# A hybrid GLA/MLA encoder layer: the order of the first loads, eight places in the last projection sweep's timetable, and the maxima at both edges of attention

## The chip, the cores and the metric

The kernel runs on one core of one Trainium2 chip. The core has five engines with a queue each: TensorE (PE, matmuls and transposes), VectorE (DVE), ScalarE (ACT), GpSimd (POOL) and SyncE (SP), which issues most DMAs here. Each queue runs in order. The metric is the device time of one execution in microseconds (us); the time of a kernel is the median of its runs.

## The reference, cut to what matters

One encoder layer on a sequence of 2048 positions and a model width of 1024, all in float32:

```
h = x @ w_in                                   # one projection, columns split between two groups
group A: bidirectional gated linear attention (4 heads), per-head RMSNorm, times silu(gate)
group B: cq, ckv, kr, gate                     # 256, 128, 64 and 512 columns of h
  q = rms_norm(cq) @ w_uq, k_nope and v from rms_norm(ckv) @ w_ukv, rotary parts of q and kr
  s = q_nope . k_nope + q_rope . k_rope        # (query, key) scores, no mask
  p = softmax(s);  o = p @ v;  o * silu(gate)
out = layer_norm(alpha * x + concat(A, B) @ w_out)
```

The softmax is taken as exp(s - max s) over its sum, so each block of queries needs the maximum over all keys before its first exponential.

## The kernel before, in words

**Split numbers.** Every product is made of three matmuls: an operand is split into a high part (`hi`, L364, an ACT copy into the matmul type) and a low part (`lo`, L371, the difference, on DVE or POOL), and high*high, high*low and low*high are added in PSUM (`mm3`, L419).

**Sweep A** (`sweep_a`, L616) goes over the 16 chunks of 128 positions from the last to the first and makes group A's chunked attention. At its head the transposed x of chunk 15 is loaded in two halves and split, then 13 pieces of the weights of A follow in three column groups (`A_GROUPS`: 288, 384 and 384 columns), each split as it lands; `ident`, `wgf` (the gate's second weight) and `wgm` (a column of factors) are loaded behind the second group; `wg` is made from them on DVE (L669). Then x of chunk 14 is loaded and split. All these splits stand in one order per engine (`worder`). The first chunk's three products run in `step(0, ...)`; `lr` (the low-rank gate input) comes from the first, `lrT` is its transpose, `z` (L891) the gate product, which needs `lrTs` and `wg`, and `za` the chain of ACT and DVE steps behind it. The tiles of these steps (pool `g1`) lie in the memory that the weight stage (`sta`) leaves.

**Sweep C** (`sweep_c`, L1100) goes over the chunks again, two to a step, eight steps, and makes group B's projections and finishes group A. Its order is a timetable: every action has a place (step + offset in `PLACE_C`; `PLACE_C_FIRST` and `PLACE_C_LAST` replace it for the first and last step), all actions are sorted by place, and each engine's queue follows that order. A pair of offsets is for the even and the odd chunk of a step. The actions that matter here: `xh` and `xl` (high and low part of x of a chunk, into one of the two halves of `xch` and `xcl`; `xl` is on POOL), `ipa` to `ipd` (the mixed projection of a chunk in four parts of six matmuls, into `ipm`; in the last 8 of the 24 the low part of x is read), `pz` (the gate product of a step in eight parts, which reads both halves of `xch` and `xcl`), `gm1` to `gm4` (its silu: three ACT steps and one on DVE), `Ob` (the state part of group A's output, PE, which reads `MMb` and `qlb` that POOL makes), `og` (DVE, the last reader of `Ob`), `krfa` (POOL, the key's rotary sum), `krsh` (ACT, its high part), `pq` (the queries' product). `pz`, `Ob` and `pq` share two PSUM buffers in turn (tag `gp`), so each waits for the last reader of the one before the last.

The weights of sweep C (`load_ws`, L459) are split in eight pieces; high and low parts and the raw pieces share 17 buffers.

**Attention** (`attention`, L1507) has 16 blocks (4 heads times 4 blocks of 512 queries); each takes the 2048 keys in 8 score tiles of two PSUM banks. It also runs by places (`PLACE`, `PLACE_LAST` for the last block; the unit is one score tile): `scores` (10 matmuls into one of two buffers `pS`), `copy` (ACT, to `s` in SBUF), `smax` (DVE, two maxima of 512 columns into `rm`), at the block's end `tmax` (PE transposes), `rmax` (DVE), `bmax` (PE, spreads the maximum into `mb`), then `sub` (DVE), `exp`, `phi` (ACT), `plo` (POOL) and `pv` (PE, 6 matmuls into `o`). The buffer of a score tile is free when both its copy and its maximum have read it. In block 0 the maxima read the copies; in later blocks they read PSUM:

```
                src = s if i == 0 else ps
```

The output projection follows; its first matmuls (`po`) use the `pS` buffers that the last block leaves.

Of the kernel before, what the change touches and what calls it, by code (L numbers as in the profile page):

```python
# [9 lines left out]
F32 = mybir.dt.float32  # L10
# [85 lines left out]
    yc=16.9,  # L96
)
PLACE_LAST = dict(
    sub=(9.67, 8.74, 8.38, 6.77, 10.45, 3.53, 9.53, 5.55),
    exp=(10.14, 9.35, 10.49, 8.31, 13.01, 14.59, 17.1, 18.05),  # L100
# [158 lines left out]
    MMl=(-0.109, 0.558),  # L259
    krfa=(-0.119, 0.94),  # L260
    krsl=(0.252, 1.09),
# [9 lines left out]
    gm1=0.643,  # L271
    gm2=0.686,
    gm3=0.706,
    gm4=0.804,
    sgm=1.056,
# [10 lines left out]
    ipd=(0.042, 0.445),  # L286
    Ob=(-0.03, 0.299),
    tm=(0.495, 1.083),
# [30 lines left out]
    qrTl=(1.081, 2.186),  # L319
    xl=(-0.244, 0.038),  # L320
    M=(-0.531, -0.11),
# [35 lines left out]
class K:  # L357
# [100 lines left out]

    def load_ws(self, pool, srcs, ncols, tag, on_pool=()):  # L459


        names = lambda p: [f"{tag}{p}{k}" for k in range(NK)]
        raw = [pool.tile([P, ncols], F32, tag=tag, name=n) for n in names("r")]
        for r, src in zip(raw, srcs):
            self.w_load = self.nc.sync.dma_start(r, src).ins
        yield
        wh = [pool.tile([P, ncols], F32R, tag=tag, name=n) for n in names("h")]
        W = []
        for k, n in enumerate(names("l")):
            wl = pool.tile([P, ncols], F32R, tag=tag, name=n)  # L470
            self.hi(wh[k], raw[k])
# [144 lines left out]
    def sweep_a(self):  # L616
        tc, nc, ins, cp = self.tc, self.nc, self.ins, self.cp
        with ExitStack() as ctx:
# [6 lines left out]
            rmask = wp.tile([P, H, P], F32, name="rmask")  # L625
            wgm = wp.tile([98, 1], F32, name="wgm")
            wg = wp.tile([98, H, P], F32R, name="wg")
# [17 lines left out]
            with tc.tile_pool(name="sta", bufs=1, reuse_waits="tile") as sta:  # L645
                xf = self.load_x(NCH - 1, "xa", 1, 2)
                xcur = self.split_x(xp, xf, NCH - 1, "xa", "dve", 2)
                wgf = sta.tile([98, H * P], F32, name="wgf")
                wgh = sta.tile([98, H * P], F32R, name="wgh")
                wdone, worder = [], {}  # L650
                for g, (c0, n) in enumerate(A_GROUPS):
                    k = 0
                    for m in W_PIECES[g]:
                        st = sta.tile([P, m, n], F32, name=f"was{g}_{k}")
                        nc.sync.dma_start(st, ins[f"wA{g}"][:, k:k + m])
                        ks, cs = slice(k, k + m), slice(c0, c0 + n)
                        with self.in_order(worder):
                            for e in [slice(j, j + 1) for j in range(m)] if g == 0 else [slice(0, m)]:
                                kh, kl = wah[:, ks, cs][:, e], wal[:, ks, cs][:, e]
                                ops = self.hi(kh, st[:, e]), self.lo(kl, st[:, e], kh)  # L660
                        k += m
                        wdone.append(ops)
                    if g == 1:
                        nc.sync.dma_start(self.ident, ins["ident"])
                        nc.sync.dma_start(wgf, ins["wg"])
                        nc.sync.dma_start(wgm, ins["wgm"])
                with self.in_order(worder):
                    self.hi(wgh, wgf)
                    nc.vector.scalar_tensor_tensor(wg.rearrange("p h d -> p (h d)"), wgh.bitcast(F32), wgm[:, 0:1],  # L669
                                                   wgf, ALU.mult, ALU.add)  # L670
                xnext = self.split_x(xp, self.load_x(NCH - 2, "xa", 1, 2), NCH - 2, "xa", "dve", 2)
                nc.sync.dma_start(rmask, ins["rmask"])
                nc.sync.dma_start(mask, ins["mask"])
# [8 lines left out]
            run = lambda n, i: [0 for _ in getattr(self, "ga_" + n)(ch[i])]  # L682
            ch[0]["x"], ch[1]["x"] = xcur, xnext

# [14 lines left out]
            self.first_lr = wdone[7][0]  # L699
            step(0, {(1, 7): [("lrT", "cur")]})  # L700
            run("bst", 0)
# [42 lines left out]
    def products(self, d, g, after=lambda g, k: None):  # L744

        nc, c, i, g1 = self.nc, d["c"], d["i"], d["g1"]
        c0, n = A_GROUPS[g]
        xh, xl = d["x"]
        if i == 0 and g == 2:
            pt = self.gp.tile([P, 1024], F32, tag="gp", name=f"ipa{c}_{g}")  # L750
        else:
            pt = self.ip.tile([P, 512], F32, tag="ip", name=f"ipa{c}_{g}")
        d["pt", g] = pt
        for k in range(NK):
            wh, wl = self.wa[k]
            self.mm3(pt[:, :n], xh[:, k, 0], xl[:, k, 0], wh[:, c0:c0 + n], wl[:, c0:c0 + n],
                     start=(k == 0), stop=(k == NK - 1))
            if k < NK - 1:
                after(g, k)
            yield k  # L760
        if i == 0 or i > 3:
            for n in (("lr", "q2"), ("k2", "v1"), ("v3",))[g]:
                for _ in getattr(self, "ga_" + n)(d):
                    pass
# [303 lines left out]
    def late_gates(self):  # L1068
# [7 lines left out]
        self.wabs_l = bc.tile([P, 2, H, P], F32R, name="wabs_l")  # L1076
        wm = self.load_ws(self.wm, [ins["wB"][k, :, 512:960] for k in range(NK)], 448, "wm")
        wz = self.load_ws(self.wz, [ins["wB"][k, :, 960:1472] for k in range(NK)], 512, "wz")
        next(wm)
# [427 lines left out]
    def attention(self):  # L1507
# [4 lines left out]
        with ExitStack() as ctx:  # L1512
# [19 lines left out]

            def scores(i, j):


                d = stt[i]
                qh, ql, rh, rl = d["q"]
                ps = d["ps", j] = pS.tile([P, 2, QB], F32, tag="pS", name=f"pS{i}_{j}")
                for e in range(2):
                    kh, kl, kr = (t[:, 2 * j + e, :P] for t in (self.ckvT_h, self.ckvT_l, self.kr))  # L1540
# [11 lines left out]
            def smax(i, j):  # L1552

                d = stt[i]
                s = d["s"][j]
                ps = d.pop(("ps", j))
                src = s if i == 0 else ps
                if j == 0:
# [408 lines left out]
def layouts(inputs):  # L1967
# [19 lines left out]
    wg, bg = wg.reshape(32, H * P), bg.reshape(1, H * P)  # L1987
    a["wg"] = np.concatenate([wg, wg, wg, bg, bg], axis=0)
    wgm = np.zeros((98, 1), np.float32)
    wgm[64:96] = -1.0  # L1990
    wgm[97] = -1.0
    a["wgm"] = wgm
    a["gn_col"] = g["gla_norm_g"][0].reshape(P, 1)
# [41 lines left out]
```

## Time and profile before

| | us |
|---|---|
| median of 3 runs (lowest, highest) | 1308.29 (1307.52, 1310.21) |
| the profiled execution | 1306.76 |
| its span, first to last instruction | 1304.7 |
| PE busy | 1284.8 |
| DVE, ACT, POOL busy | 961.9, 817.2, 785.9 |

Sweep A fills the span to about 370 us, sweep C to about 610, attention to about 1130, and the output projection the rest. A row of the timeline has the start, the duration, engine, source line, operation, written and read tile, shape and count, and in brackets the idle time of the engine before it with what ended it. In the view of waits a row has the total, the count and the longest wait. The rows of stretches have, for each engine, the busy time and in parentheses the number of instructions, then the granted TensorE clock, the DMA share and the GB/s. A busy PE is not PE at its peak: matmuls overlap, and the idle times counted before them are a little shorter than the distance that the starts show.

### The profile page before, as it was taken

To read this page: it belongs to the slowest core of one execution; us is meant where nothing else is said; L and a number is where in the kernel's file an instruction comes from. 1 tells how busy PE (TensorE), PEld (TensorE's weight loads), DVE (VectorE), ACT (ScalarE), POOL (GpSimd) and SP (SyncE) were. 2 spreads that over 40 slices of the span, in tenths; PEclk is the share of its full clock that TensorE was granted. 3 is DMA by queue.
4 is the path that set the end of the run, shared out by engine and by line. 5 is a ranking of instruction groups with operands and counts; after the bars stand their busy time and mean duration, and the time that the engine had idled before them with its cause. 6 is when DMAs were issued, how large, how long until landed. Compare 5 with 4: busy or idle time off the path is not lost.

```text
span 1304.7 us, 19969 instructions
## 1 busy us (share of the span) xinstructions
PE 1284.8 (98%) x7082; PEld 1131.1 (87%) x7082; DVE 961.9 (74%) x1706; ACT 817.2 (63%) x1334; POOL 785.9 (60%) x494
## 2 busy tenths in 40 slices
PE   7999999999999999999999999999999999999997
PEld 7999999999999999999788888888888887888886
DVE  6966675656675555555888888888888888469997
ACT  6765655566676566564778787878888888511110
POOL 0143333242467667661488888889999999844441
PEclk9999999999999999999999999999999999999999
DMA  8132313131475555656301111121123210366662
GB/s 285 62 101 54 94 53 94 49 88 59 155 247 194 187 178 200 207 176 209 90 1 41 41 42 41 41 62 60 57 71 101 47 41 9 121 203 202 214 196 97
DMA packets 105908, 145.81 MB, mean 112 GB/s; under 512 B 16743, under 2 KB 59375, under 8 KB 105809
## 3 DMA queue, kind: packets, MB, share of 16 engines
q1 hardware_dynamic: 97744, 142.41, 34.8%
q0 software_dynamic: 672, 2.10, 0.4%
q8 instruction: 56, 0.92, 0.3%
q10 hardware_dynamic: 7392, 0.03, 0.3%
q14 instruction: 44, 0.35, 0.1%
HBM read 94.14 MB, written 50.36 MB: 111 GB/s over the span
## 4 chain that ended last, share of the span: by engine, by line
PE 91%; DVE 2%; ACT 2%; issue 1%; POOL 0%; SPq 0%; DMA 0%; DVEq 0%; ACTq 0%
PE pz L1210 7%; PE ipm L1281 5%; PE o L421 5%; PE o L423 5%; PE o L422 5%; PE pS L1541 4%; PE pS L1544 4%; PE pS L1543 4%; PE pS L1545 4%; PE pS L1542 4%; PE ipa L421 4%; PE ipa L422 4%; PE ipa L423 4%; PE po L421 2%; PE po L423 2%; PE po L422 2%
## 5 line engine op out<-in xcount | busy, mean ns | idle before, releaser
L373 POOL TENSOR_TENSOR pl<-s,ph 128x1024 fp32r<-128x1024 f32 x128 | 307.0, 2413 | 67.0 <-ACT ph L367 61.7
L1563 DVE TENSOR_TENSOR rm<-pS,rm 128x512 f32<-128x512 f32 x210 | 144.9, 690 | 44.7 <-ACT s L1550 39.6
L1550 ACT ACTIVATE s<-pS 128x1024 f32<-128x1024 f32 x128 | 131.4, 1027 | 68.2 <-PE pS L1545 66.2
L1587 DVE TENSOR_TENSOR s<-s,mb 128x1024 f32<-128x1024 f32 x128 | 151.2, 1213 | 9.1 <-PE mb L1581 9.0
L1039 POOL TENSOR_TENSOR Us<-Us,cw 128x512 f32<-128x512 f32 x16 | 20.0, 1248 | 228.5 <-DVE Us L1037 190.0
L367 ACT ACTIVATE ph<-s 128x1024 fp32r<-128x1024 f32 x128 | 135.0, 1056 | 18.3 <-PE o L423 17.8
L1591 ACT ACTIVATE s<-s 128x1024 f32<-128x1024 f32 x128 | 131.4, 1050 | 13.4 <-DVE s L1587 13.4
L421 PE MATMUL ipa<-wah,xah 128*128 128x384 f32 (+1 forms) x384 | 130.0, 339 | 6.5 <-ACT wah L367 6.4
L422 PE MATMUL ipa<-wal,xah 128*128 128x384 f32 (+1 forms) x384 | 125.7, 327 | 0.0
L423 PE MATMUL ipa<-wah,xal 128*128 128x384 f32 (+1 forms) x384 | 125.2, 326 | 0.0
L1541 PE MATMUL pS<-qh,ckvT_h 128*128 128x512 f32 x256 | 103.7, 405 | 0.7 <-ACT s L1591 0.4
L421 PE MATMUL o<-ph,vh 128*128 128x512 f32 x256 | 102.6, 401 | 0.0
L423 PE MATMUL o<-ph,vl 128*128 128x512 f32 x256 | 101.3, 396 | 0.0
L1544 PE MATMUL pS<-rh,krs 128*128 128x512 f32 x256 | 101.2, 395 | 0.0
L422 PE MATMUL o<-pl,vh 128*128 128x512 f32 x256 | 101.1, 395 | 0.0
L1543 PE MATMUL pS<-qh,ckvT_l 128*128 128x512 f32 x256 | 100.9, 394 | 0.0
L1545 PE MATMUL pS<-rl,krs 128*128 128x512 f32 x256 | 100.7, 393 | 0.0
L1542 PE MATMUL pS<-ql,ckvT_h 128*128 128x512 f32 x256 | 100.6, 393 | 0.0
L1614 DVE TENSOR_TENSOR ap<-ap,s 128x512 f32<-128x512 f32 x120 | 83.1, 693 | 2.7 <-ACT s L1591 0.8
L373 POOL TENSOR_TENSOR ol<-of,oh 128x512 fp32r<-128x512 f32 x32 | 43.0, 1345 | 64.7 <-ACT oh L367 64.7
L421 PEld LDWEIGHTS ipa<-wah,xah 128*128 128x128 f32 x384 | 73.4, 191 | 7.6 <-ACT wah L367 6.8
L422 PEld LDWEIGHTS ipa<-wal,xah 128*128 128x128 f32 x384 | 73.5, 191 | 0.9 <-DVE wal L373 0.4
(325 smaller groups left out, 3839.4 us busy)
## 6 DMA issues: line engine op xcount, KB each, us to landing
xcf<-xT_dram SPq DMA_DIRECT2D x16, 512.0 KB, 5.4
xr<-x_dram SPq DMA_DIRECT2D x16, 512.0 KB, 5.3
out_dram<-rr SPq DMA_DIRECT2D x32, 256.0 KB, 2.0
xaf<-xT_dram SPq DMA_DIRECT2D x14, 512.0 KB, 4.3
oib<-oi_s SPq DMA_DIRECT2D x16, 256.0 KB, 4.0
qdb<-qd_s SPq DMA_DIRECT2D x16, 256.0 KB, 4.2
SU<-su_s SPq DMA_DIRECT2D x16, 256.0 KB, 4.4
ub<-u_s SPq DMA_DIRECT2D x16, 256.0 KB, 4.6
```

The source lines that it names most:

```text
L367: return nc.scalar.activation(dst, src, AF.Copy).ins
L373: return e.tensor_tensor(dst, src, hi.bitcast(F32), ALU.subtract).ins
L421: mm(out, ah, bh, start=start, stop=False)
L422: mm(out, ah, bl, start=False, stop=False)
L423: mm(out, al, bh, start=False, stop=stop)
L1541: mm(ps[:, e], kh, qh, start=True, stop=False)
L1542: mm(ps[:, e], kh, ql, start=False, stop=False)
L1543: mm(ps[:, e], kl, qh, start=False, stop=False)
L1544: mm(ps[:, e], kr, rh, start=False, stop=False)
L1545: mm(ps[:, e], kr, rl, start=False, stop=True)
L1563: V.tensor_tensor(d["rm"], src[:, e], d["rm"], ALU.max)
L1587: V.tensor_tensor(s, s, d["mb"][:, None, :].to_broadcast([P, 2, QB]), ALU.subtract)
```

## The change

1. **First loads.** The halves of chunk 15's x are loaded and split in the weights' order: first half, two weight pieces, second half, two pieces. `wgm` becomes a 513th column of `wg`'s input, so its DMA goes, and `wgf` is loaded behind all weight pieces. x of chunk 14 is loaded behind it; its split is written down after the first chunk's step. In that step `lrT` comes after the sixth k of the second product instead of after the eighth, and the copy `q2` after the second product instead of the first.
2. **`load_ws`**: all eight high parts are written down ahead of the low parts.
3. **Sweep C's places.** First step: `krfa` of chunk 0 later (behind `MMl`, `qlb` of chunk 0 and `Sf2` of chunk 1 on POOL); `gm2` to `gm4` later (behind `xh` of chunk 2 on ACT; `gm4` behind `og` of chunk 0 on DVE). Last step: `Ob` of chunk 14 behind `ipc` of chunk 14 on PE; `xl` of chunk 15 later (behind `qlb`, `MMl` and `krfa` of chunk 15 on POOL). Its new place, 7.64, lies behind `ipc` and `ipd` of chunk 15 (7.42, 7.445) and the first two parts of the last `pz` (7.572, 7.578) and ahead of the third (7.707): those products now read the low part that chunk 13 left in that half of `xcl`, and the third part of `pz` reads the new one.
4. **Attention's edges.** The last maximum of block 0 (tile 7) reads PSUM and stands ahead of its copy; `bmax` of block 0 goes between the two halves of block 1's second score tile, which is put down as two halves of five matmuls; the maxima of block 1's first four tiles read the copies. In block 15 the last maximum stands ahead of its copy, and that copy goes behind `phi` of (14, 5) and the copy `yc` of block 13 on ACT.

```diff
+PLACE_FIRST = dict(bmax=2.01, max=(1.21,) * 7 + (0.72,))
 PLACE_LAST = dict(
+    max=(1.21,) * 7 + (0.72,),
+    copy=(0.73,) * 7 + (1.0,),
...
-    krfa=(-0.119, 0.94),
+    krfa=(-0.02, 0.94),
...
-    gm2=0.686,
-    gm3=0.706,
-    gm4=0.804,
+    gm2=0.815,
+    gm3=0.82,
+    gm4=0.83,
...
-    Ob=(-0.03, 0.299),
+    Ob=(0.0, 0.299),
...
-    xl=(-0.244, 0.038),
+    xl=(-0.244, 0.64),
...
+        if high_first:
+            for h, r in zip(wh, raw):
+                self.hi(h, r)
         for k, n in enumerate(names("l")):
             wl = pool.tile([P, ncols], F32R, tag=tag, name=n)
-            self.hi(wh[k], raw[k])
+            if not high_first:
+                self.hi(wh[k], raw[k])
...
+                        if g == 0 and k in (0, NK // 2):
+                            xs = slice(k, k + NK // 2)
+                            nc.sync.dma_start(xf[:, xs], ins["xT"][NCH - 1][:, xs])
+                            with self.in_order(worder):
+                                self.hi(xcur[0][:, xs, 0], xf[:, xs])
+                                self.lo(xcur[1][:, xs, 0], xf[:, xs], xcur[0][:, xs, 0])
...
                     if g == 1:
                         nc.sync.dma_start(self.ident, ins["ident"])
-                        nc.sync.dma_start(wgf, ins["wg"])
-                        nc.sync.dma_start(wgm, ins["wgm"])
+                nc.sync.dma_start(wgf, ins["wg"])
                 with self.in_order(worder):
-                    self.hi(wgh, wgf)
-                    nc.vector.scalar_tensor_tensor(wg.rearrange("p h d -> p (h d)"), wgh.bitcast(F32), wgm[:, 0:1],
-                                                   wgf, ALU.mult, ALU.add)
-                xnext = self.split_x(xp, self.load_x(NCH - 2, "xa", 1, 2), NCH - 2, "xa", "dve", 2)
+                    self.hi(wgh, wgf[:, :H * P])
+                    nc.vector.scalar_tensor_tensor(wg.rearrange("p h d -> p (h d)"), wgh.bitcast(F32),
+                                                   wgf[:, H * P:], wgf[:, :H * P], ALU.mult, ALU.add)
+                xnext = self.load_x(NCH - 2, "xa", 1, 2)
...
-            step(0, {(1, 7): [("lrT", "cur")]})
+            step(0, {(1, 5): [("lrT", "cur")]})
+            ch[1]["x"] = self.split_x(xp, xnext, NCH - 2, "xa", "dve", 2)
...
-            for n in (("lr", "q2"), ("k2", "v1"), ("v3",))[g]:
+            for n in ((("lr", "q2"), ("k2", "v1"), ("v3",)) if i else (("lr",), ("q2", "k2", "v1"), ("v3",)))[g]:
...
-                src = s if i == 0 else ps
+                src = s if NP * i + j < NP - 1 or NP <= NP * i + j < NP + 4 else ps
...
-                p = PLACE_LAST.get(f, PLACE[f]) if i == nb - 1 else PLACE[f]
+                p = {nb - 1: PLACE_LAST, 0: PLACE_FIRST}.get(i, {}).get(f, PLACE[f])
...
-                    put(t, scores, i, j)
+                    if (i, j) == (1, 1):
+
+                        put(t, scores, i, j, (0,))
+                        put(t + 0.02, scores, i, j, (1,))
+                    else:
+                        put(t, scores, i, j)
```

More of the change, by code (lines that the diff above doesn't have):

```diff
@@ L457, in load_w, with load_ws @@
         return wh, wl
-    def load_ws(self, pool, srcs, ncols, tag, on_pool=()):
+    def load_ws(self, pool, srcs, ncols, tag, on_pool=(), high_first=False):
         names = lambda p: [f"{tag}{p}{k}" for k in range(NK)]
@@ L625, in sweep_a @@
             rmask = wp.tile([P, H, P], F32, name="rmask")
-            wgm = wp.tile([98, 1], F32, name="wgm")
             wg = wp.tile([98, H, P], F32R, name="wg")
@@ L645, in sweep_a @@
             with tc.tile_pool(name="sta", bufs=1, reuse_waits="tile") as sta:
-                xf = self.load_x(NCH - 1, "xa", 1, 2)
-                xcur = self.split_x(xp, xf, NCH - 1, "xa", "dve", 2)
-                wgf = sta.tile([98, H * P], F32, name="wgf")
+                xf = self.xfp.tile([P, NK, P], F32, tag="xf", name=f"xaf{NCH - 1}", bufs=2)
+                xcur = [xp.tile([P, NK, 1, P], F32R, tag=f"x{p}", name=f"xa{p}{NCH - 1}", bufs=2) for p in "hl"]
+                wgf = sta.tile([98, H * P + 1], F32, name="wgf")
                 wgh = sta.tile([98, H * P], F32R, name="wgh")
@@ L682, in sweep_a @@
             run = lambda n, i: [0 for _ in getattr(self, "ga_" + n)(ch[i])]
-            ch[0]["x"], ch[1]["x"] = xcur, xnext
+            ch[0]["x"] = xcur
             def step(i, steps):
@@ L1076, in late_gates @@
         self.wabs_l = bc.tile([P, 2, H, P], F32R, name="wabs_l")
-        wm = self.load_ws(self.wm, [ins["wB"][k, :, 512:960] for k in range(NK)], 448, "wm")
-        wz = self.load_ws(self.wz, [ins["wB"][k, :, 960:1472] for k in range(NK)], 512, "wz")
+        wm = self.load_ws(self.wm, [ins["wB"][k, :, 512:960] for k in range(NK)], 448, "wm", high_first=True)
+        wz = self.load_ws(self.wz, [ins["wB"][k, :, 960:1472] for k in range(NK)], 512, "wz", high_first=True)
         next(wm)
@@ L1531, in fetch, with scores @@
                         nc.sync.dma_start(q[-1][r].bitcast(F32), src[h])
-            def scores(i, j):
+            def scores(i, j, es=(0, 1)):
                 d = stt[i]
                 qh, ql, rh, rl = d["q"]
-                ps = d["ps", j] = pS.tile([P, 2, QB], F32, tag="pS", name=f"pS{i}_{j}")
-                for e in range(2):
+                if es[0] == 0:
+                    d["ps", j] = pS.tile([P, 2, QB], F32, tag="pS", name=f"pS{i}_{j}")
+                ps = d["ps", j]
+                for e in es:
                     kh, kl, kr = (t[:, 2 * j + e, :P] for t in (self.ckvT_h, self.ckvT_l, self.kr))
@@ L1555, in smax @@
                 s = d["s"][j]
-                ps = d.pop(("ps", j))
-                src = s if i == 0 else ps
+                ps = d["ps", j]
+                src = s if NP * i + j < NP - 1 or NP <= NP * i + j < NP + 4 else ps
                 if j == 0:
@@ L1987, in layouts @@
     wg, bg = wg.reshape(32, H * P), bg.reshape(1, H * P)
-    a["wg"] = np.concatenate([wg, wg, wg, bg, bg], axis=0)
+    wg = np.concatenate([wg, wg, wg, bg, bg], axis=0)
     wgm = np.zeros((98, 1), np.float32)
@@ L1991, in layouts @@
     wgm[97] = -1.0
-    a["wgm"] = wgm
+    a["wg"] = np.concatenate([wg, wgm], axis=1)
     a["gn_col"] = g["gla_norm_g"][0].reshape(P, 1)
```

## The prediction

> **What bounds the kernel now.** I read the busy times of the page first.
>
> ```profile
> span 1304.7 us, 19969 instructions
> ## 1 busy us (share of the span) xinstructions
> PE 1284.8 (98%) x7082; PEld 1131.1 (87%) x7082; DVE 961.9 (74%) x1706; ACT 817.2 (63%) x1334; POOL 785.9 (60%) x494
> ```
>
> TensorE is the bound: 1304.7 - 1284.8 = 19.9 us of the span are all that it does not work. The change removes no matmul, so it can only move these holes or make new ones. PE's rows in the view of waits say where they are:
>
> ```profile
> PE ipa L421 <- ACT wah L367: 6.4, 2, 6.0
> PE mx L1569 <- DVE rm L1563: 0.9, 2, 0.6
> PE mb L1581 <- DVE mc L1574: 0.8, 1, 0.8
> PE z L891 <- ACT lrTs L367: 0.7, 1, 0.7
> PE Ob L1439 <- POOL qlb L373: 0.6, 1, 0.6
> ...
> PE pS L1541 <- ACT s L1591: 0.4, 1, 0.4
> PE pS L1541 <- DVE rm L1563: 0.3, 1, 0.3
> ```
>
> The start holds 6.4; below it single waits under 1 us stand at just the places that the change touches. So I go from place to place, and ask at each what is late next. Rows of the timeline, by engine, carry this.
>
> **Start.** ACT, DVE, PE, and then the stretches of PE's `ipa` matmuls:
>
> ```profile
> 4.64 0.63 ACT L367 ACTIVATE xah<-xaf 128x512 fp32r<-128x512 f32 x1 [0.31 <-DMA xaf<-xT_dram]
> 5.46 0.78 ACT L367 ACTIVATE wah<-was 128x288 fp32r<-128x288 f32 x2 [0.19 <-DMA was<-wA_dram]
> ```
> ```profile
> 20.01 1.14 ACT L367 ACTIVATE xah<-xaf 128x512 fp32r<-128x512 f32 x2
> 21.38 0.60 ACT L367 ACTIVATE q<-ipa 128x512 f32<-128x512 f32 x1 [0.24 <-DVE wg L669]
> ```
> ```profile
> 16.80 3.89 DVE L373 TENSOR_TENSOR wal<-was,wah 128x768 fp32r<-128x768 f32 x5 [0.88 <-ACT wah L367]
> 20.60 0.74 DVE L669 SCALAR_TENSOR_TENSOR wg<-wgh,wgm,wgf 98x512 fp32r<-98x512 f32 x1
> ```
> ```profile
> 22.85 0.66 PE L891 MATMUL z<-lrTs,wg 98*128 98x128 f32 x4 [0.74 <-ACT lrTs L367]
> ```
> ```profile
> 8.40:13.20 4.80, 4.72 (x18) 4.52 (x19) 0.00 (x0) 0.00 (x0) 1.00 1.03 351
> 13.20:17.50 4.30, 4.30 (x25) 4.18 (x24) 0.18 (x1) 0.27 (x2) 1.00 1.04 365
> ```
>
> The first weight's high part starts at 5.46, behind the second half of x at 4.64; with their order exchanged it can start 5.46 - 4.64 = 0.8 sooner, and so the first matmul. All bytes still come, though, and the last weights set when the first product ends. What leaves their way is `wgf`: 98 x 512 x 4 = 200,704 bytes, at the second stretch's 365 GB/s an estimated 0.55 us. So DVE's low parts (16.80 + 3.89 = 20.69) end 0.55 sooner, at 20.14; `wg` is now last behind them, 0.74, and done at about 20.9. The copies of `q`, `k`, `VV` and `lrTs` lie in memory of the weight stage and so wait for `wg`'s end, as the row at 21.38 shows; PE's 0.74 at `z` is their last, `lrTs`. With `lrT` earlier, `z` can come soon after 20.9 instead of at 22.85. But PE's next work is chunk 14's product, and its x, whose split (1.14 on ACT, as much on DVE) stood ahead of these copies, is now written down behind the step. If ACT gets it done while it waits for `wg`, product and `z` are both sooner, by an estimated 1.3 at most (the 1.14, and about half of the 0.24 that ACT waited); if it comes behind the copies (from 20.9 some 1.8, then 1.14, so till 23.8), PE waits there for what it gained at `z`, and may lose up to 0.4. Of -1.3 to +0.4 I take **-0.5**, what the loads alone give. In `load_ws` the high parts come ahead of lows that ACT need no longer wait for; matmuls without a hole cover this: **0**; uncovered, `gm1` would be what gains or loses, and it waits for PE.
>
> **Sweep C, first step.** ACT, then PE:
>
> ```profile
> 394.05 1.04 ACT L367 ACTIVATE xch<-xcf 128x1024 fp32r<-128x1024 f32 x1
> ```
> ```profile
> 395.61 0.35 PE L1438 MATMUL Ob<-MMb,qhb 128*128 128x256 f32 x1 [0.31 <-DVE gm L1224]
> ```
>
> `Ob` of chunk 1 needs the `gp` buffer that `gm4` reads last, and PE already waits 0.31 for it. The change puts ACT's copy of chunk 2 (1.04) ahead of `gm2` and `gm3`, so `gm4` ends 1.04 later and nothing else is late first: **+1.0**. Ends: 0 if something else holds `Ob` of chunk 1 as long already, which the 0.31 put down to `gm` speaks against, and +1.3 if `og` of chunk 0, now ahead of `gm4` on DVE, holds that too.
>
> **Sweep C, last step.** The two waits of `Ob` on PE:
>
> ```profile
> 577.75 0.33 PE L1439 MATMUL Ob<-MMb,qlb 128*128 128x128 f32 x1 [0.64 <-POOL qlb L373]
> ...
> 583.56 0.39 PE L1438 MATMUL Ob<-MMb,qhb 128*128 128x256 f32 x1 [0.42 <-POOL MMb L373]
> ```
>
> Both go: 0.64 (chunk 14, six `ipc` matmuls now stand ahead of it) and 0.42 (chunk 15, whose `qlb` and `MMl` lose `xl`'s place ahead of them on POOL). What is late next, on DVE and PE:
>
> ```profile
> 586.45 1.13 DVE L1465 SCALAR_TENSOR_TENSOR og<-Ob,rg_r,ub 128x128 f32<-128x128 f32 x4
> ```
> ```profile
> 588.19 0.28 PE L421 MATMUL pq<-cqT_h,wabs_h 128*128 128x256 f32 x1
> ```
>
> `og` of chunk 14 ends at 586.45 + 1.13 = 587.58, and `pq`, which needs its `gp` buffer, starts at 588.19, only 0.61 behind. PE would reach `pq` 1.06 sooner and then wait 1.06 - 0.61 = 0.45; and as `Ob` of chunk 14, moved behind `ipc`, starts `og`'s chain later by those matmuls, most of the 0.61 goes too. I take **-0.2**; ends -1.06 and 0.
>
> `xl` of chunk 15 is the new cost. POOL's `xl` (of chunk 14's place; all have one shape) and `krfa` of chunk 15, then PE in the last `pz`:
>
> ```profile
> 578.34 2.41 POOL L373 TENSOR_TENSOR xcl<-xcf,xch 128x1024 fp32r<-128x1024 f32 x1
> ```
> ```profile
> 594.38 0.33 POOL L1315 TENSOR_TENSOR krf<-krf,rope 128x64 f32<-128x64 f32 x1 [4.67 <-DVE rope L1490]
> ```
> ```profile
> 595.50 0.28 PE L1210 MATMUL pz<-xcl,wzh 128*128 128x256 f32 x1
> ...
> 595.86 0.28 PE L1210 MATMUL pz<-xcl,wzh 128*128 128x256 f32 x1
> ```
>
> `xl` overwrites the half of `xcl` that the first two parts of `pz` read, so POOL can't begin before the last of these reads, at 595.50, is over (595.78); the third part's first read of `xcl` is at 595.86 and now needs `xl`'s result. 595.78 + 2.41 = 598.2; PE's queue has nothing between that can go on, so the hole is 598.2 - 595.86 = 2.3, and an estimated 0.2 for two hand-overs: **+2.5**. `krfa`, put ahead of `xl`, ends at 594.71, in time. Ends: 0, if the third part isn't held, and 2.9, with hand-overs of 0.3 each (the smallest waits of the rows above). In the first step `krfa` of chunk 0 only changes its place among POOL's work (0.33 for such a sum); `krsh` on ACT waits for it, and `tm` on PE later still: **0**, up to 0.3 either way if `tm` were what PE meets next.
>
> **Attention's first edge.** DVE, PE, then a stretch (PE, PEld, DVE, ACT, POOL, busy us and instructions):
>
> ```profile
> 640.09 1.42 DVE L1563 TENSOR_TENSOR rm<-pS,rm 128x512 f32<-128x512 f32 x2 [0.40 <-ACT s L1550]
> ...
> 648.20 2.21 DVE L1563 TENSOR_TENSOR rm<-pS,rm 128x512 f32<-128x512 f32 x3
> ```
> ```profile
> 650.54 0.39 PE L1541 MATMUL pS<-qh,ckvT_h 128*128 128x512 f32 x1
> ```
> ```profile
> 635.00:649.20 14.20, 13.49 (x58) 10.38 (x57) 13.60 (x17) 14.06 (x15) 8.90 (x4) 1.00 0.01 1
> ```
>
> By the waits shown first, the edge's holes are 0.3 (`mx`, 0.9 less the 0.6 of the last edge), 0.8 (`mb`), 0.4 and 0.3 (`pS`): 1.8, and an estimated 2.5 with the 0.2 by which, at the `mx` below, a hole lengthens the distance of starts, for each of four. The change fills `mb`'s with half a score tile and takes the maximum away from `mx`'s path. What limits next is the exponentials' side: ACT works 14.06 of the 14.2 from 635.0 on, and DVE 13.60, so `sub`, `exp` and the copies don't come sooner than their own sum lets them; the maximum of (1, 4) at 648.20, which still reads PSUM, frees a buffer that PE takes at 650.54, 0.9 behind the 649.6 at which its two operations (1.4) end. So PE gains no more than that 0.9 and the little by which the chain starts sooner. And the copy of tile 7 now comes after its maximum, where 640.09 shows the reverse wait (0.40 for the copy of the same tile): the two are never side by side on one tile. I take **-1.0**; ends -2.5 and -0.3 (`mx`'s hole alone). The Trainium skill, "PSUM — Partial Sum Buffer", section "PSUM bank collisions raise a hardware error", says that two engines must not touch one bank at a time, reads among it; the trace agrees as far as the 0.40 goes. Were copy and maximum free to overlap, by that page's rule undone, the sum's -1.0 would be an estimated -1.2, and the time 1309.1.
>
> **Attention's last edge.** DVE and PE:
>
> ```profile
> 1100.16 1.42 DVE L1563 TENSOR_TENSOR rm<-pS,rm 128x512 f32<-128x512 f32 x2 [0.90 <-ACT s L1550]
> ```
> ```profile
> 1100.69 0.40 PE L423 MATMUL o<-ph,vl 128*128 128x512 f32 x1
> 1101.72 0.63 PE L1569 MATMUL mx<-ident,rm 128*128 128x128 f32 x4 [0.64 <-DVE rm L1563]
> ```
>
> The maximum of (15, 7) no longer waits 0.90 for its copy, so `mx`'s 0.64 goes (0.8 by starts: 1101.72 - 1100.69 = 1.03, less the 0.2 or so that lies between overlapping matmuls' starts): **-0.8**, ends -0.8 and 0. The copy, now behind a high part and `yc`, is due only at its `sub` and at `po`, which needs the buffer after many `pv`.
>
> **Sum:** -0.5 + 1.0 - 0.2 + 2.5 - 1.0 - 0.8 = +1.0. On the profiled execution (1306.76, that is its span and 2.06 around it) this gives 1307.8. The median of the runs, 1308.29, is 1.53 above that execution; on it the sum gives **1309.3**.
>
> **Rivals.** *No hole at `xl`.* If the third part of `pz` is not held, the sum loses 2.5, and with DVE a little ahead at `og` a further 0.86: +1.0 - 2.5 - 0.9 = -2.4, 1305.9; with the start's and the first edge's better ends (-0.8, -1.5) as far as 1303.6. For it: all gains stand where the waits are. Against: both `pz` rows read `xcl`, and one matmul has 256 columns, which are both chunks. Chance 0.23.
>
> *The hole slows what follows it* (the other side). In the stretch from 8.40, behind the 6.0 us wait, 18 matmuls of 288 columns took 4.72; at the second stretch's 4.30 for 25 of 384 they would have taken 18 x 288 x 4.30 / (25 x 384) = 2.3. So PE runs at half its pace for some 4.7 us after a long hole, though the granted clock shows 1.00 in both rows. Price 2.4, 1311.7; it decides if more than 1.6 of it comes. Against it: no hole of about 1 us later in the trace is followed by such matmuls, and 2.5 is nearer to these than to 6. Chance 0.15. The Trainium skill, "TensorE: Matmul & The Clock Gate", section "Part 1: The HAM clock gate (the "warmup" mystery)", gives half clock after an idle window of about 3.4 us, and as long for getting out of it: by that page 2.5 us of idle would not do.
>
> *The change doesn't do what it says at the start*: the split of chunk 14's x comes behind the copies and PE waits for it instead, +0.4 for -0.5; with the first edge giving its 0.3 alone, since PE waits at (1, 5) and (1, 6) for what it gained before, the sum is +1.0 + 0.9 + 0.7 = +2.6, 1310.9, on the border of slower. Chance 0.12.
>
> **How the numbers follow.** A measurement of this kernel can tell about 0.2%, 2.6 us. Forecast 0.50, its own range 1307.0 to 1310.9 (start and first edge each at an end). Faster: three quarters of the first rival and 0.03 of the forecast's tail, 0.20. Slower: the second rival and half the third, with 0.04 of the forecast's tail, 0.25. The rest, 0.55, is within. The range cuts about one in ten at each side: from 1304.4, inside the first rival, to 1312.4, the second with the start at its bad end.
>
> **What would show it.** After: a hole of 2.4 us on PE at a `pz` matmul put down to POOL `xcl`; `Ob` of chunk 1 waiting 1.3 for `gm`; no wait at the two last `Ob` but one at `pq` for `og`; no `mb` and `mx` waits, and new ones on `pS` until about 650; `z` at about 22.3. The prediction is wrong if `xl` comes between without a hole, if matmuls behind it run at half pace, or if a wait appears at a place not named here.

## The result, and the profile after

| | median us (lowest to highest, runs) | ratio to the kernel before (95% interval) |
|---|---|---|
| before | 1307.90 (1306.64 to 1310.21, 4) | |
| changed | 1316.64 (1315.10 to 1317.86, 4) | 1.0067 (1.0053 to 1.0082) |

The change costs 8.7 us, on the slower side and above the range of the prediction (1304.4 to 1312.4). The span of the profiled execution went from 1304.7 to 1314.0, 9.3 more.

The head of the changed kernel's page:

```profile
span 1314.0 us, 19954 instructions
## 1 busy us (share of the span) xinstructions
PE 1289.5 (98%) x7082; PEld 1133.8 (86%) x7082; DVE 970.1 (74%) x1706; ACT 816.6 (62%) x1334; POOL 789.5 (60%) x494
```

PE's busy time is 4.7 us longer for the same 7082 matmuls, so some of them ran slower; the idle time grew from 19.9 to 24.5, another 4.6. PE's rows in the view of waits say where the second half is:

```profile
PE ipa L424 <- ACT wah L370: 5.0, 1, 5.0
PE pS L1555 <- ACT ph L370: 3.7, 1, 3.7
PE pz L1222 <- DVE wzl L376: 2.5, 1, 2.5
PE pz L1222 <- POOL xcl L376: 2.2, 1, 2.2
PE pqr L424 <- ACT oT L1487: 0.8, 1, 0.8
```

Of the kernel before's waits, those at `mx` (last edge), `mb`, `z` and `Ob` are gone, as meant. In their place stand three of over 2 us. The third, for `xcl`, was forecast; the one for `wzl` and the one at `pS` were not. The slower matmuls are found by stretches (PE, PEld, DVE, ACT, POOL, then the granted clock): just behind the wait for `wzl`, just behind that for `xcl`, just behind that at `pS`, and a little later.

```profile
380.10:381.50 1.40, 1.34 (x6) 1.34 (x7) 1.40 (x6) 0.37 (x2) 1.40 (x3) 0.50 0.00 0
599.90:601.00 1.10, 1.04 (x8) 1.04 (x9) 0.00 (x0) 0.00 (x0) 0.00 (x1) 1.00 0.55 178
657.40:659.00 1.60, 1.54 (x4) 1.28 (x5) 1.55 (x3) 1.60 (x2) 1.60 (x2) 0.50 0.00 0
665.00:667.00 2.00, 2.00 (x10) 1.63 (x9) 0.85 (x2) 1.94 (x3) 1.69 (x1) 1.00 0.00 0
```

Behind two of the three holes the granted clock is 0.50. A ledger shows what each place is worth. It compares the start of the same matmul in both traces (after less before), and so adds up to what PE has lost by then:

| up to | after less before | step | what lies there |
|---|---|---|---|
| 358.71 (`Op`, end of sweep A) | -1.75 | -1.75 | the start |
| 378.5 to 384.5 (`pz`, first step of C) | +2.3 | +4.0 | hole for `wzl` 2.5, then 1.5 at half clock |
| 395.61 (`Ob` of chunk 1) | +1.75 | -0.5 | its wait for `gm` is gone |
| 577 to 594 (last step of C) | +1.7 | 0.0 | `Ob`'s waits gone (-1.1), a new one for `oT` (+1.1) |
| 595.86 (`pz`) | +4.09 | +2.4 | hole for `xcl` |
| 648 (first edge) | +2.7 | -1.4 | `mx`, `mb`, `pS` |
| 650.54 (`pS`, tile (1, 6)) | +6.9 | +4.2 | the hole at `pS` |
| 655 | +9.6 | +2.7 | half clock behind it |
| 1101.72 (`mx`, last edge) | +8.8 | -0.8 | the last edge |
| 1250 | +9.2 | +0.4 | output projection |

So most gains came about; two holes that the prediction did not have, with the clock behind them, are 4.0 + 6.9 = 10.9 us.

**Where the two holes come from.** Both lead to DVE. The low parts of the last weights, eight operations of one shape, before and after:

```profile
371.58 5.99 DVE L373 TENSOR_TENSOR wzl<-wzr,wzh 128x512 fp32r<-128x512 f32 x8
```
```profile
369.02 11.08 DVE L376 TENSOR_TENSOR wzl<-wzr,wzh 128x512 fp32r<-128x512 f32 x8
```

They begin 2.6 us sooner and end 2.5 later. The last two of them, and what POOL did at that time in the changed kernel:

```profile
374.85 5.25 DVE L376 TENSOR_TENSOR wzl<-wzr,wzh 128x512 fp32r<-128x512 f32 x2
```
```profile
374.29 1.37 POOL L1427 TENSOR_TENSOR SU<-Sf,cw 64x512 f32<-64x512 f32 x1
375.73 1.37 POOL L1419 TENSOR_TENSOR Sf<-Sf,cw 64x512 f32<-64x512 f32 x1
377.07 1.27 POOL L376 TENSOR_TENSOR MMb<-SU,MMb 128x512 fp32r<-128x512 f32 x1
378.30 1.25 POOL L376 TENSOR_TENSOR qlb<-qdb,qhb 128x512 fp32r<-128x512 f32 x1
```

Two operations that take 0.69 each alone last from 374.85 to 380.10. The single operations end 0.55 behind a POOL operation: POOL's row ends at 375.66 and the first of them at 376.2, POOL's at 379.55 and the last at 380.10. The last began at 376.3 and lasted 3.81, through three operations of POOL (those at 375.73, 377.07 and 378.30) that follow each other without a gap. The same picture at attention's first edge, DVE and POOL of the changed kernel:

```profile
644.30 2.81 DVE L1577 TENSOR_TENSOR rm<-s,rm 128x512 f32<-128x512 f32 x2 [0.26 <-ACT s L1564]
647.03 2.35 DVE L1601 TENSOR_TENSOR s<-s,mb 128x1024 f32<-128x1024 f32 x2
649.29 3.50 DVE L1577 TENSOR_TENSOR rm<-s,rm 128x512 f32<-128x512 f32 x2
652.71 2.15 DVE L1628 TENSOR_TENSOR ap<-ap,s 128x512 f32<-128x512 f32 x3
...
655.90 2.21 DVE L1577 TENSOR_TENSOR rm<-pS,rm 128x512 f32<-128x512 f32 x3
```
```profile
643.44 2.39 POOL L376 TENSOR_TENSOR pl<-s,ph 128x1024 fp32r<-128x1024 f32 x1 [12.69 <-ACT ph L370]
646.91 5.33 POOL L376 TENSOR_TENSOR pl<-s,ph 128x1024 fp32r<-128x1024 f32 x2 [1.07 <-ACT ph L370]
652.20 2.82 POOL L1631 TENSOR_TENSOR acc<-s,s 128x1024 f32<-128x1024 f32 x1
```

Compare the rows of one shape, 128x512: two maxima from the copies (`s`) take 2.81 and 3.50 beside POOL's work, three maxima from PSUM (`pS`) 2.21, three sums into `ap` (which lies in PSUM) 2.15. Also `s<-s,mb`, with `mb` in PSUM, isn't held up. POOL's rows are longer too: 5.33 for two low parts that take 2.4 each. So what is held up is a DVE operation with both inputs in SBUF that starts beside a POOL operation, and it is held up until that operation ends. From this came theory P of the runs.

### The profile page after: what moved, and what is told of

It reads as the page before. It is cut to its first block, busy times and chain, and to the rows that moved or that the text cites. A ratio compares the mean times of both kernels' runs of the same rounds, so it can differ in the third digit from the quotient of the medians.

```text
span 1314.0 us, 19954 instructions
## 1 busy us (share of the span) xinstructions
PE 1289.5 (98%) x7082; PEld 1133.8 (86%) x7082; DVE 970.1 (74%) x1706; ACT 816.6 (62%) x1334; POOL 789.5 (60%) x494
## 4 chain that ended last, share of the span: by engine, by line
PE 85%; DVE 5%; DMA 2%; ACT 2%; issue 1%; POOL 1%; SPq 0%; DVEq 0%; POOLq 0%; ACTq 0%
PE pz L1222 7%; PE ipm L1293 6%; PE o L425 4%; PE o L424 4%; PE o L426 4%; PE pS L1555 4%; PE pS L1558 4%; PE pS L1557 4%; PE pS L1556 4%; PE pS L1559 4%; PE ipa L424 4%; PE ipa L425 4%; PE ipa L426 4%; PE ipg L424 2%; PE ipg L426 2%; PE ipg L425 2%
## 5 line engine op out<-in xcount | busy, mean ns | idle before, releaser
L1577 DVE TENSOR_TENSOR rm<-pS,rm 128x512 f32<-128x512 f32 x206 | 142.1, 690 | 45.2 <-ACT s L1564 39.9
L1051 POOL TENSOR_TENSOR Us<-Us,cw 128x512 f32<-128x512 f32 x16 | 19.9, 1247 | 226.7 <-DVE Us L1049 188.3
L1222 PE MATMUL pz<-xch,wzl 128*128 128x256 f32 x256 | 72.3, 286 | 2.5 <-DVE wzl L376 2.5
```

What stands on the lines that cost most here:

```text
L1222: self.nc.tensor.matmul(s["pz"][:, h], self.Wz[k][w][:, h * P:(h + 1) * P], x2(x, k), start=(k == 0 and p == 0), stop=stop.get(h) == (k, p))
L1577: V.tensor_tensor(d["rm"], src[:, e], d["rm"], ALU.max)
```

## Experiments

**Two theories for `wzl`, two for `pS`.** P: a DVE operation with two SBUF inputs and a POOL operation hold each other up. H: the order of `load_ws` alone makes the lows late. C: at `pS`, ACT's copies or high parts, to which the profile puts the wait, are late by themselves.

### One part undone at a time

`a1`, the order of `load_ws`:

```diff
-..., 448, "wm", high_first=True)
-..., 512, "wz", high_first=True)
+..., 448, "wm")
+..., 512, "wz")
```

> The changed kernel with the order of load_ws as before (each low part behind its high part), nothing else. The changed kernel's PE waits 2.5 us for the last wzl, whose DVE operation took 3.81 us (alone 0.69) while POOL ran three operations. Theory P (a DVE operation with two SBUF inputs and a POOL operation hold each other up): the lows keep the distance of 0.60 instead of 0.78 and the last one comes up to 1.3 us sooner against POOL's work; the wait at pz shrinks to between 0 and 1.5, and the clock's fall behind it (1.5 us) goes: 2.5 to 4.0 us faster, 1312.6 to 1314.1. Rival H (the lows' own order is the whole cause, POOL nothing): the last lows take 0.7 each and the wait goes wholly, 4.0 us faster.

`a2`, `krfa` of chunk 0:

```diff
-    krfa=(-0.02, 0.94),
+    krfa=(-0.119, 0.94),
```

> The changed kernel with krfa of chunk 0 at its old place on POOL (ahead of MMl and qlb), nothing else. Theory P: POOL then stops behind Sf, since krfa waits for DVE's rope, which stands behind the lows; the last wzl is held up by Sf alone and takes about 1.3 instead of 3.81, the 2.5 us wait at pz falls below 0.3 and the half clock behind it doesn't come: about 4 us faster, 1312.6. Rival H (the lows' order alone): krfa's place changes nothing at pz, within 0.3 us of 1316.6.

`a3`, the maxima of block 1's first tiles:

```diff
-src = s if NP * i + j < NP - 1 or NP <= NP * i + j < NP + 4 else ps
+src = s if NP * i + j < NP - 1 else ps
```

> The changed kernel with the maxima of block 1's first four tiles reading PSUM again as before; halves and places of the edge stay. Theory P: the two maxima that took 2.08 and 2.78 us beside POOL's low parts take 0.69 each again (one input in PSUM), so the 3.7 us wait at pS and the half clock behind it (2.7 us) go, and one or two waits of 0.3 to 0.5 for the maxima's buffers come back: 5.4 to 6.4 us faster, 1310.2 to 1311.2. Rival C (the copies or the high parts on ACT, to which the profile puts that wait, are late by themselves): the wait of 3.7 stays, within 1 us of 1316.6.

`a4`, `xl` of chunk 15:

```diff
-    xl=(-0.244, 0.64),
+    xl=(-0.244, 0.038),
```

> The changed kernel with xl of chunk 15 at its old place, nothing else. By the prediction's step the hole of 2.2 us at the last pz goes; what it gave at Ob of chunk 15 (0.4) comes back in part: 1.8 to 2.4 us faster, 1314.2 to 1314.8. Rival: the wait at pqr for oT (0.8) is due to xl's absence from POOL's queue and goes as well: 3.0 us faster.

| | median us | ratio to before (95%) | less than changed |
|---|---|---|---|
| changed | 1316.64 | 1.0067 (1.0053 to 1.0082) | |
| a1 | 1313.60 | 1.0040 (1.0026 to 1.0055) | 3.0 |
| a2 | 1313.23 | 1.0044 (1.0027 to 1.0061) | 3.4 |
| a3 | 1311.72 | 1.0025 (1.0011 to 1.0038) | 4.9 |
| a4 | 1314.35 | 1.0048 (1.0033 to 1.0063) | 2.3 |

In `a1` and in `a2` the wait for `wzl` is gone altogether, so the hole needs both parts. `a1` alone does not separate P from H, which both expected it faster. `a2` decides against H, which expected no effect of `krfa`: the order of `load_ws` is still the new one there. DVE, then POOL of `a2`:

```profile
368.50 8.63 DVE L376 TENSOR_TENSOR wzl<-wzr,wzh 128x512 fp32r<-128x512 f32 x8
```
```profile
375.22 1.37 POOL L1419 TENSOR_TENSOR Sf<-Sf,cw 64x512 f32<-64x512 f32 x1
378.14 0.32 POOL L1327 TENSOR_TENSOR krf<-krf,rope 128x64 f32<-128x64 f32 x1 [1.56 <-DVE rope L1502]
```

POOL stops for 1.56 us because `krfa` waits for `rope`, which stands behind the lows on DVE; in that gap the last low gets through. What looked like a mere change of order on POOL was the pause that let DVE finish. The lows still take 8.63 instead of 5.99: some of that is POOL's doing, some the new order, in which each low starts only when the one before has ended.

`a3` decides against C. The maxima of the same tiles, DVE, and what PE then waits for:

```profile
647.49 1.42 DVE L1577 TENSOR_TENSOR rm<-pS,rm 128x512 f32<-128x512 f32 x2 [0.27 <-ACT s L1564]
648.82 2.34 DVE L1601 TENSOR_TENSOR s<-s,mb 128x1024 f32<-128x1024 f32 x2
651.08 1.41 DVE L1577 TENSOR_TENSOR rm<-pS,rm 128x512 f32<-128x512 f32 x2
```
```profile
646.24 0.47 PE L1555 MATMUL pS<-qh,ckvT_h 128*128 128x512 f32 x1 [1.51 <-DVE rm L1577]
```

Two maxima take 1.4 again, the hole of 3.7 is gone and with it the half clock behind it; a wait of 1.5 for a maximum stands in its place, larger than the 0.3 to 0.5 expected, and the 4.9 us won fall short of the 5.4 to 6.4. The wait for `wzl` is still there, as in the changed kernel: 2.1 and then 0.9, with the half clock behind them. `a4` gave what was expected (2.3), but PE's waits show that `xl` at its old place costs `Ob` of chunk 15 more than before, and that the wait for `oT` is not `xl`'s doing (it is absent in `b2`, `b3` and `d1` below, where `Ob` of chunk 14 has its old place):

```profile
585.05 0.38 PE L1450 MATMUL Ob<-MMb,qhb 128*128 128x256 f32 x1 [1.05 <-POOL MMb L376]
...
588.68 0.38 PE L424 MATMUL pqr<-wqr_h,cqT_h 128*128 128x256 f32 x1 [0.78 <-ACT oT L1487]
```

### The suspected cause far from the edges

`c1` puts the disputed input into the kernel before, in the middle of attention:

```diff
-                src = s if i == 0 else ps
+                src = s if i == 0 or (i == 5 and j < 4) else ps
```

> The kernel before with one edit, far from any edge: in block 5 the maxima of the first four tiles read the copies instead of PSUM (seven maxima get two inputs in SBUF). POOL is busy there nearly all the time. Theory P: these rows of DVE take up to 0.69 + 2.4 us instead of 0.69, POOL's low parts beside them up to 0.7 longer; DVE loses 5 to 15 us in the block, PE waits for the score buffers and the kernel is 3 to 12 us slower. Rival C (what cost time at the edge was the late copies, not the maxima's input): the rows stay at 0.69 and the time within 1 us of the kernel before.

Measured: 1315.81 against 1307.41, ratio 1.0060 (1.0045 to 1.0076), 8.4 us slower by seven operations that got another input. DVE, POOL and PE of that block:

```profile
763.15 3.63 DVE L1563 TENSOR_TENSOR rm<-s,rm 128x512 f32<-128x512 f32 x2
766.70 1.21 DVE L1587 TENSOR_TENSOR s<-s,mb 128x1024 f32<-128x1024 f32 x1
767.84 5.67 DVE L1563 TENSOR_TENSOR rm<-s,rm 128x512 f32<-128x512 f32 x2
```
```profile
763.83 2.41 POOL L373 TENSOR_TENSOR pl<-s,ph 128x1024 fp32r<-128x1024 f32 x1 [3.04 <-ACT ph L367]
767.78 2.41 POOL L373 TENSOR_TENSOR pl<-s,ph 128x1024 fp32r<-128x1024 f32 x1 [1.55 <-ACT ph L367]
770.61 2.36 POOL L373 TENSOR_TENSOR pl<-s,ph 128x1024 fp32r<-128x1024 f32 x1 [0.41 <-POOL pl L373]
```
```profile
776.42 0.80 PE L421 MATMUL o<-ph,vh 128*128 128x512 f32 x1 [5.27 <-DVE ofl L373]
```

In the second pair each maximum waits for one of POOL's operations: 767.84 + 5.67 = 773.5, 0.5 behind the end of POOL's at 772.97. PE then waits 5.3 for DVE, which is late by what it lost, and the clock is 0.50 behind the hole. P is shown: neither ACT's copies nor an edge is needed.

### What is left without the losses

The next four kernels are the changed one with parts undone, as their expectations say.

> The changed kernel with four parts undone: the order in load_ws, krfa's and xl's places in sweep C, and the maxima of block 1 from the copies. What stays: the start, gm2 to gm4, Ob of chunk 14, the edge of block 0 (maximum ahead of its copy, halves) and the last edge. By the traces of the four runs before: start -1.6, the place of gm -0.4, Ob -0.9 and the wait for oT +0.8, the first edge -1.5 and a wait of 1.2 for a maximum, the last edge -0.7: -3.1, 1304.4. If instead the losses share a cause that these parts only bring to light (rival: the first edge or the start makes DVE and POOL meet), one of the waits of 2 us or more stays and the time is above 1307.

> As the run before, and the first edge of attention and Ob's place undone as well: start, gm2 to gm4 and the last edge are what is left of the change. From the traces: -1.6 - 0.4 - 0.7 = -2.7, 1304.8, by the new order of the first edge being worth nothing net. If the first edge is worth the 1.0 that the prediction gave it, this is 0.7 to 1.0 slower than the run before.

> Only the start's part of the change, all else as before. Traces: every row of PE behind the first product 1.1 to 1.9 us earlier in the changed kernel and its variants: 1305.7 to 1306.4. The prediction's step: -0.5, 1307.0.

> As the first of these runs, but the maxima of block 1's first two tiles still read the copies (in the changed kernel these ran before POOL's first low part and took 0.69 each). Theory P: no DVE operation is held up by POOL; the maxima of tiles 0 and 1 free their buffers a little sooner; within 0.5 us of the first of these runs. Rival: copies as the maxima's input cost DVE time by themselves, whatever POOL does: 1 to 3 us slower than it.

| | median us | ratio to before (95%) |
|---|---|---|
| before, beside these | 1307.45 | |
| b1: four parts undone | 1306.85 | 0.9996 (0.9987 to 1.0005) |
| b2: start, `gm`, last edge | 1304.97 | 0.9980 (0.9971 to 0.9989) |
| b3: start alone | 1306.28 | 0.9996 (0.9987 to 1.0005) |
| b4: as b1, two maxima from copies | 1306.30 | 0.9994 (0.9986 to 1.0003) |

`b2` came out as expected, and is faster than the kernel before. `b1` missed: expected 1304.4. None of the waits over 2 us stays in it, so the losses were those four parts; what the expectation lacked stands in its trace. In sweep C's first step 1.3 of the start's gain is given back, most of it at `Ob` of chunk 0, which waits for `qlb`; `Ob` of chunk 14 with the old `xl` nets to +1.1; the first edge nets to nothing (-1.6 by the end of `mb`, then +1.5, most of it at the wait for a maximum); and +1.2 lies in the output projection (a wait of 0.97 for `rt`). The cause of the last stays open; `c1`, which has none of the change's parts, loses 1.4 there too. `b4` isn't told apart from `b1`: two maxima from copies, ahead of POOL's first low part, are not held up (1.41 for two in its trace), and do not help either, as PE then waits 1.9 for an exponential.

`b3`'s ratio, with an interval from 1.7 us faster to 0.7 slower, doesn't say how much the start gives by itself. Its trace has 1.8 at the end of sweep A, and shows where part of it goes, in sweep C's first step:

```profile
381.85 0.33 PE L1449 MATMUL Ob<-MMb,qlb 128*128 128x128 f32 x1 [0.81 <-POOL qlb L374]
```

PE comes sooner, but `qlb` of chunk 0 on POOL doesn't, so 1.1 of the start's gain is given back there. The new place of `krfa`, behind `qlb`, should return it; that was the last run.

```diff
 # the kernel before, with the start's part and:
+    krfa=(-0.02, 0.94), gm2=0.815, gm3=0.82, gm4=0.83          # PLACE_C_FIRST
+    max=(1.21,) * 7 + (0.72,), copy=(0.73,) * 7 + (1.0,)       # PLACE_LAST
```

> The parts that the traces show as gains, together: the start, krfa of chunk 0 and gm2 to gm4 at their new places in sweep C, the last edge; load_ws, Ob, xl and the first edge as before. With krfa behind them, MMl and qlb are ready when Ob of chunk 0 wants them, so the 0.8 that it waited for qlb in the runs with krfa undone goes: 0.8 to 1.1 faster than start, gm and last edge alone (1304.97), 1303.9 to 1304.2. Rival: without the order in load_ws, POOL's unbroken row of work holds up the last lows on DVE all the same; then pz waits for wzl and the gain is 0 or less.

Measured: 1305.07 (1303.62 to 1306.53), ratio 0.9982 (0.9973 to 0.9991). In its trace the wait at `Ob` of chunk 0 is gone, and no `pz` waits for `wzl`: PE is 2.3 us ahead at chunk 1's `Ob`, where `b2` was level; of this difference 1.1 is the wait and 1.3 a better start in that one execution. But the 0.8 to 1.1 expected over `b2` did not come: the medians are 0.1 apart, with intervals of about 1.2 to each side. The start itself varies from execution to execution by as much (in the ten traces with the new start it is worth between 0.6 and 2.3 at the end of sweep A; the two with the old one differ by 0.6), so the two kernels aren't told apart. Both beat the kernel before by about 2.4 us, and the changed one by about 11.6.

## Why the prediction was wrong

**Start, -0.5.** Right in sign, too small: -1.75. Most of it, 1.68, is there when the first product ends, where the prediction allowed the loads 0.55; in the other traces with the new start that point lies from 2.0 sooner to 0.4 later, and what decides it stays open. The steadier part is `z`, which comes another 0.7 to 0.9 sooner in all ten. There the split of chunk 14's x went neither wholly ahead of the copies nor wholly behind them. ACT, then PE of the changed kernel:

```profile
19.17 0.64 ACT L370 ACTIVATE xah<-xaf 128x512 fp32r<-128x512 f32 x1
20.13 0.28 ACT L370 ACTIVATE lrTs<-lrT 98x128 fp32r<-98x128 f32 x1 [0.33 <-DVE wg L680]
```
```profile
20.46 0.66 PE L903 MATMUL z<-lrTs,wg 98*128 98x128 f32 x4
21.43 0.65 PE L974 MATMUL kT<-ident,k 128*128 128x128 f32 x4 [0.31 <-ACT k L370]
21.84 0.38 PE L424 MATMUL ipa<-wah,xah 128*128 128x288 f32 x1
```

Its first half fills ACT's wait for `wg`, `lrTs` comes first behind it, and `z` is 2.4 sooner, at 20.46; the second half stands behind the copies and is still in time. Of the gain at `z`, 0.2 to 1.0 is left at chunk 14's product. The -1.3 of the prediction was for the whole split ahead of the copies. Alone (`b3`) the start's ratio, 0.9996, is near the -0.5, by luck if at all: the interval holds zero, and 1.1 of 1.8 goes where the prediction did not look, to the wait for `qlb` on POOL.

**`load_ws`, 0, and `krfa`, 0.** These are the steps that failed first: put at nothing, they cost +4.0 together. The prediction looked for waits, found PE without a hole, and named `gm1` as what would be late if the cover went. It did not ask what the lows meet on DVE when they run at another time: the spacing of the lows and POOL's chain moved against each other, and POOL lost the pause that `krfa`'s wait gave. Either part alone costs no wait.

**`gm2` to `gm4`, +1.0.** Wrong in sign: -0.5. `gm4` did come later, but `Ob` of chunk 1 no longer waits for it. DVE and PE of the changed kernel:

```profile
397.26 1.23 DVE L1236 TENSOR_TENSOR gm<-pz,gm 128x1024 f32<-128x1024 f32 x1 [3.49 <-issue]
```
```profile
397.36 0.28 PE L1450 MATMUL Ob<-MMb,qhb 128*128 128x256 f32 x1
```

`Ob` is written while `gm4` still reads `pz`, so it isn't in `pz`'s buffer. With `og` of chunk 0 ahead of `gm4`, the buffer of chunk 0's `Ob` comes free first, and it seems to be the one that is given out; that last step is argued from these two rows, not tried. The prediction, and the description ahead of it, took the two buffers as a fixed turn.

**`Ob`, -0.2.** Near in size: -1.1 and +1.1. That a later `Ob` takes the gain back was right, but the next limit was not `og` at `pq`: it was `oT` on ACT at `pqr`, which the same chain behind the moved `Ob` makes late.

**`xl`, +2.5.** Right: a wait of 2.24 and a step of 2.4, behind a `xl` of 2.34 that starts when `pz`'s first parts are done. POOL and PE of the changed kernel:

```profile
597.57 2.34 POOL L376 TENSOR_TENSOR xcl<-xcf,xch 128x1024 fp32r<-128x1024 f32 x1 [1.16 <-PE pz L1222]
```
```profile
599.96 0.38 PE L1222 MATMUL pz<-xcl,wzh 128*128 128x256 f32 x1 [2.24 <-POOL xcl L376]
```

**First edge, -1.0.** The step that failed most: -1.4 until 648, then +4.2 and +2.7. The prediction gave the maxima of four tiles from the copies no price at all. Its terms are the holes that go and DVE's full queue, and its 1.4 for two maxima is from a row that reads PSUM. In block 0, where the maxima read the copies, POOL hardly works (1.30 of the 20 us from 612 to 632). But the one operation that it does there stood in the trace of before with its effect. DVE, then POOL:

```profile
623.21 1.42 DVE L1563 TENSOR_TENSOR rm<-s,rm 128x512 f32<-128x512 f32 x2 [0.92 <-ACT s L1550]
625.95 1.70 DVE L1563 TENSOR_TENSOR rm<-s,rm 128x512 f32<-128x512 f32 x2 [1.32 <-ACT s L1550]
```
```profile
625.08 1.30 POOL L373 TENSOR_TENSOR wv_l<-wvf,wv_h 128x512 fp32r<-128x512 f32 x1 [15.36 <-ACT wv_h L367]
```

The pair that starts beside it takes 1.70 instead of 1.42. In block 1 POOL is busy 8.90 of the 14.2 us from 635.0 on, and every DVE operation there has an operand in PSUM. The Trainium skill, "SBUF — State Buffer", sections "Who interferes with whom" and "Summary: rules for kernel authors", says it outright: a DVE instruction with two SBUF inputs contends with a GpSimd instruction that reads SBUF, and the second one to issue is blocked fully until the first finishes. The runs agree: 2.81 and 3.50 instead of 1.4 for two. The prediction drew on the rule on PSUM banks here, worth 0.2, and not on this one. Even without the hold-ups (`a3`, `b1`) the edge gives nothing net: a maximum in DVE's full queue, the kind of limit that the prediction named but at an earlier tile, takes back the 1.6 gained, where the prediction left it 0.9 of spare.

**Last edge, -0.8.** Right: -0.8 in every trace that has it.

**The rival of the slowed matmuls** came true, but mostly elsewhere. Behind the `xl` hole of the changed kernel's profiled execution, and of `a2`'s, the clock stayed at 1.00; in `a1` and `a3` it fell there and cost 1.6 and 1.5. Behind the two holes that the prediction did not have it fell to 0.50. Its price, 2.4, was about right: 1.5 and 2.7. The direction that the prediction gave most of its chance to was missed because two terms of the sum were put at 0 and -1.0 that measured +4.0 and +5.5.

## What to carry to other kernels

When an operand or a place in a queue changes, ask of each DVE operation where its inputs lie and what POOL runs at that moment; a duration from a row is only good for the company in which it was measured. A wait on an engine that is off the path can be what lets another engine through: removing the wait can cost more than it held. Where PE is the bound, a hole of 2 us or more may cost half as much again or more through the clock behind it, by where it happens to lie, and the order in which buffers come free is as much a part of a timetable as the order of the work.

## What the runs showed of the hardware

A DVE operation with two SBUF inputs that starts beside a POOL operation took up to 2.9 us instead of 0.69 (`c1`), and 3.81 where POOL's operations follow each other without a gap: it waits for all three. One PSUM input is enough to be free of it (two maxima from PSUM beside POOL took 1.41 in `a3`). It goes the other way too: in the changed kernel a low part of POOL that starts at 649.36, just behind a maximum from the copies, took 2.88 instead of 2.41.

The granted clock fell to 0.50 behind some holes of PE and not behind others. By the distance of starts over the hole: 1.9 to 2.3, none of three (`a3` and `b1` at `pS`, `b4`); 2.33, with another of 1.34 close behind it, one of one (`wzl` of `a3`); 2.5 to 2.75, three of six (yes at `wzl` of the changed kernel and at `xl` of `a1` and `a3`; no at `xl` of the changed kernel and of `a2`, nor at `wzl` of `a4`); 4.1 and more, five of five. Once down it stayed for 3.4 or 6.8 us.

Length alone doesn't decide; the place does. In each of the six traces that have a fall within the kernel, every fall and rise of the clock there lies on one grid of 3.413 us (in the changed kernel at 379.90, 383.32, 656.38 and 663.21, for example: 1, 81 and 83 steps from the first). Counted by these slots, the clock fell at the end of every slot in which PE was busy for 1.44 us or less, and of none in which it was busy for 1.81 or more; between these there was no case. (That holds for all twelve traces, the other six counted from the fall at their end; the first 30 us are left out, as the rows there show 1.00 where PE goes at half its pace.) Behind a fall it rose after one slot where PE was busy for 3.1 us or more of it, and after two where for 2.7 or less. So one and the same hole for `xl`, 2.24 us idle, falls mostly into one slot in `a1` and is cut by a slot's border in the changed kernel. The slots that hold most of it, the changed kernel's and then `a1`'s with the slot behind it (PE, PEld, DVE, ACT, POOL, then the clock):

```profile
598.36:601.77 3.41, 1.81 (x15) 1.81 (x16) 0.00 (x0) 0.00 (x0) 1.54 (x1) 1.00 0.64 217
```
```profile
594.40:597.81 3.41, 1.17 (x10) 1.05 (x9) 0.00 (x0) 0.19 (x2) 2.31 (x1) 1.00 0.90 301
597.81:601.22 3.41, 3.41 (x18) 3.41 (x17) 1.14 (x6) 0.00 (x0) 0.20 (x1) 0.50 0.00 0
```

The Trainium skill, "TensorE: Matmul & The Clock Gate", section "Part 1: The HAM clock gate (the "warmup" mystery)", gives about 3.4 us of idle for the fall and a window that runs freely. The grid agrees with a free-running window; that a slot with up to 1.44 us of work in it is followed by a fall differs from its figure, and the measurement decides. What in a slot is counted, and where between 1.44 and 1.81 the border lies, stays open.
